# Offset weight buffers, earlier gating-norm loads and a later sample scaling in a one-layer decoder step

## The chip, the cores and the metric

The kernel runs on one core of one Trainium2 chip. The metric is device time in microseconds (us) of one execution. The kernel before has a median of 1687.88 us over three runs, which lie between 1686.46 and 1689.45 us. The profile comes from one more execution of the same program. In that execution the clock granted to TensorE is full throughout (0.999 in the mean).

In this text PE is TensorE, DVE is VectorE, ACT is ScalarE, POOL is GpSimd and SP is SyncE, whose queue issues most transfers. PEld is the weight-load half of TensorE. A queue name with a q, such as SPq, means the issuing of transfers on that engine.

## What is computed

The reference is one inference step of a decoder layer on 256 prompt positions and 8 sample positions, so 264 columns in all, with model width 4096. Cut to what matters here:

```
hn = rmsnorm(x, norm_gain)
p  = hn @ w_in                              # 4096 x 13324, split into 14 parts
A  = sink_attention(...) * silu(az)         # sliding window, 12 heads
B  = mlstm(...)  * sigmoid(mo) * silu(mz)   # 6 heads, matrix state
vv = layernorm(gelu(cv), c_ln_gain, c_ln_bias)
C  = gelu(cu) * (tril(w_s) @ vv + b_s) * silu(cz)
h  = x + concat(A, B, C) @ w_out            # 4096 x 4096
y  = rmsnorm(h, final_gain)                 # for the prompt and for the samples
cv_rows = vv of the last chunk              # an output of its own
```

The outputs are `y` for prompt and samples, the key and value rows, the mLSTM states, and the normalised rows `vv` of the last chunk, with scale and bias applied. All data is float32.

## The kernel before

**The matrix products.** The activations stand in SBUF as 32 rows of 264 values (one row for each 128 of the 4096 features), and they are split into a rounded part `xh` and a remainder `xl` (lines 129 and 130). Each row of `xh` and `xl` is padded from 264 to 320 values (`ROW`), which is 1280 bytes; `XOFF` is 0. The weights come in pieces of two 128x512 blocks (512 KB), also split into a rounded part `wh` and a remainder `wl`. Every product is made of three matmuls, `xh*wh`, `xl*wh` and `xh*wl`, with 128x128 weights and 264 columns. One step takes one 512 KB piece: four output blocks times two blocks of depth times three matmuls are 24 matmuls. Sixteen steps make a group of four output blocks. There are 26 groups for `w_in` and 8 for `w_out`, so 34 x 16 x 24 = 13056 main matmuls.

**How a weight piece gets there.** `load_w(n)` (line 219) issues the load of the float32 piece `wf` on SP's queue, four steps ahead. `split_w(n)` (line 228), two steps ahead, lets ACT copy it to `wh` and lets DVE subtract to give `wl`, with both of DVE's inputs in SBUF. There are three buffers each for `wf`, `wh` and `wl`. In the built program all `wh` and `wl` buffers and the rows of `xh` and `xl` start at multiples of 256 bytes in a partition, and the 128 columns of weights that one matmul takes are 512 bytes.

**What runs beside.** The rest (attention, mLSTM heads, gating, norms) is written as generators. Line 1000 starts the loop over all steps; before each output block `tick()` resumes such generators as their due times come. A due time is a `yield` with a number of microseconds, counted on a clock that the program keeps while it is written out, with estimated costs per instruction (lines 155 to 208). So the order on each engine is fixed when the program is built. Line 206 records every compute instruction, which is why nearly all rows of the profile say L206; tiles tell them apart.

**The gating part.** `gmlp_prep` (line 738) runs when the `cv` groups, the last two of `w_in`, begin. `gmlp_ln` (line 779) normalises the rows in `TM`, forms the eight gated blocks, and puts the residual `xt` back into `yb` by loads on SP's queue (lines 808, 809; line 1017 does the same for the other blocks). After that it loads the norm's scale and bias, broadcast to 128 partitions, 512 KB each, into `gb` (lines 810 to 812). POOL multiplies and adds them onto 128 and then 8 rows of `TM` (lines 815, 816), and SP's queue stores the results `o_cvp` and `o_cvs` (line 818). `gb` shares its memory with `rw`, which `gmlp_prep` uses.

**The end.** After the last matmul the sums of squares are reduced over partitions by small matmuls into `ns` (prompt) and `nss` (samples), from three tiles: `acc`, which POOL accumulates, and `last[0]` and `last[1]`, the squares of the last two blocks. `rsqrt` (line 270) is one DVE operation, a square root on ACT, and `newton`, four more on DVE. Then, for eight column blocks q, PE transposes `yb` (`turn`), ACT and DVE scale the two halves into `yo` (`put`), and SP's queue stores them (`store`). `state` and `state_out` write the mLSTM states in between. At q == 2 the samples' factor `rs` is formed and the scaled samples `yos` are stored, by SP's queue (lines 1118 to 1122).

Of the kernel before, what the change touches and what calls it, by code (L numbers as in the profile page):

```python
# [18 lines left out]
P = 128  # L19
# [50 lines left out]
LAG = 6.0  # L70
NCH = KT // KK
ROW = 320
XOFF = 0
PAD0, PAD1 = 32, 24

SM = {}
# [15 lines left out]
def body(tc, xt, wi, wg, wo, sm, kc, vc, c0, wst, w00, bs, cgain, cbias,  # L92
# [3 lines left out]
    with ExitStack() as ctx:  # L96
# [29 lines left out]
        keep = Phase("keep")  # L126

        cp.tile([P, PAD0], F32, name="pad0")
        xh = cp.tile([P, KT, ROW], F32R, name="xh")[:, :, XOFF:XOFF + T]
        xl = cp.tile([P, KT, ROW], F32R, name="xl")[:, :, XOFF:XOFF + T]  # L130
        yb = cp.tile([P, KT, T], F32, name="yb")
        sms = cp.tile([P, NSM], F32, name="sms")
        ones = cp.tile([P, P], F32, name="ones")
# [18 lines left out]
        def tt(eng, out, a, b, op):  # L152
            eng.tensor_tensor(out, a, b, op)
# [74 lines left out]
        def split_w(n):  # L228
            if n >= len(steps):
                return  # L230
            t = wf_t.pop(n)
            hi = wp.tile([P, KK, 512], F32R, name="wh")
            lo = wp.tile([P, KK, 512], F32R, name="wl")
            cur[0] = [None, clk["P"]]
            for sl in ((slice(0, 1), slice(1, 2)) if n == 0 else (slice(0, KK),)):
                A.activation(hi[:, sl], t[:, sl], AF.Copy)
                tt(V, lo[:, sl], t[:, sl], hi[:, sl].bitcast(F32), ALU.subtract)
            cur[0] = None
            wh_t[n], wl_t[n] = hi, lo
# [498 lines left out]
        def gmlp_prep():  # L738
            wm = ph.tile([P, CG, P], F32, name="wm")
            Z = ph.tile([P, CG, P], F32, name="Z")  # L740
            w0 = ph.tile([TS, CG], F32, name="w0")
            wI = ph.tile([TS, CG, TS], F32, name="wI")
            DQ.dma_start(wm, wst)
            DQ.dma_start(Z, bs.rearrange("(o g) t -> o g t", o=1).broadcast_to([P, CG, P]))
            DQ.dma_start(w0, w00.broadcast_to([TS, CG]))
            yield 6.0
            G.affine_select(out=wm, in_=wm, pattern=[[0, CG], [1, P]], compare_op=ALU.is_ge,
                            fill=0.0, base=0, channel_multiplier=-1)
            tt(V, wI, ident[:TS, :TS].unsqueeze(1).broadcast_to([TS, CG, TS]),
               w0.unsqueeze(2).broadcast_to([TS, CG, TS]), ALU.mult)  # L750
            yield
            rw = ph.tile([P, CG, P], F32, name="rw", tag="rg")
            nc.gpsimd.partition_all_reduce(rw, wm, P, ReduceOp.add)
            yield 12.0
            for g in range(CG):
                V.scalar_tensor_tensor(Z[:, g], rw[:, g], sc("cb", g), Z[:, g], ALU.mult, ALU.add)
                if g % 2:
                    yield
            st.update(wm=wm, Z=Z, wI=wI)

        def gmlp_tr(i):
            while ("gl", 4 * i + 3) not in st:
# [16 lines left out]
        def gmlp_ln():  # L779
            TM, bst, wm, Z, wI = [st[n] for n in ("TM", "bst", "wm", "Z", "wI")]  # L780
            mv = ph.tile([P, 5, 3], F32, name="mvs")
            for bb, n in ((slice(0, 2), P), (slice(2, 3), TS)):
                for b in range(bb.start, bb.stop):
                    V.bn_aggr(mv[:n, 0:2, b], bst[:n, b])
                rsqrt(mv[:n, 2, bb], mv[:n, 1, bb], 1.0, mv[:n, 3, bb], mv[:n, 4, bb])
                for b in range(bb.start, bb.stop):
                    V.tensor_scalar(TM[:n, b], TM[:n, b], mv[:n, 0, b:b + 1], mv[:n, 2, b:b + 1],
                                    ALU.subtract, ALU.mult)
            yield
            for g in range(CG):  # L790
                ps = yield from acq()
                sl = slice(P * g, P * g + P)
                PE.matmul(ps[:, 0:P], TM[:, 0, sl], wm[:, g], start=True, stop=True)
                PE.matmul(ps[:, P:TP], TM[:, 1, sl], wm[:, g], start=True, stop=True)
                PE.matmul(ps[:, TP:T], TM[:TS, 2, sl], wI[:, g], start=True, stop=True)
                s = ph.tile([P, T], F32, name="sg_s")
                V.scalar_tensor_tensor(s[:, :TP].rearrange("p (b t) -> p b t", b=2),
                                       ps[:, :TP].rearrange("p (b t) -> p b t", b=2), sc("cg", g),
                                       Z[:, g].unsqueeze(1).broadcast_to([P, 2, P]), ALU.mult, ALU.add)
                V.scalar_tensor_tensor(s[:, TP:], ps[:, TP:T], sc("cg", g),  # L800
                                       Z[:, g, 0:1].broadcast_to([P, TS]), ALU.mult, ALU.add)
                tt(V, yb[:, S_C + g], yb[:, S_C + g], s, ALU.mult)
                rel()
                split_y(S_C + g)
                st["c", g] = True
                yield NOW
                if g > 0:
                    DQ.dma_start(yb[:, S_C + g - 1, :], xt[:, S_C + g - 1, :])
            DQ.dma_start(yb[:, S_C + g, :], xt[:, S_C + g, :])
            gb = ph.tile([P, 2, 1024], F32, name="gb", tag="rg")  # L810
            DQ.dma_start(gb[:, 0], cgain.broadcast_to([P, 1024]))
            DQ.dma_start(gb[:, 1], cbias.broadcast_to([P, 1024]))
            yield 6.0
            for b, n, dst in ((1, P, o_cvp), (2, TS, o_cvs)):
                tt(G, TM[:n, b], TM[:n, b], gb[:n, 0], ALU.mult)
                tt(G, TM[:n, b], TM[:n, b], gb[:n, 1], ALU.add)
                yield
                DQ.dma_start(dst, TM[:n, b])


# [265 lines left out]
        def store(q, b, n):  # L1086
            sl = slice(512 * q, 512 * (q + n))
            DQ.dma_start(o_y[b, :, sl], yo[:, b, sl])

        turn(0, 0)  # L1090
        ns = pn.tile([P, 512], F32, name="ns", tag="sn")
        parts = [acc[:, 0]] + last
        for i, a in enumerate(parts):
            for b in range(2):
                PE.matmul(ns[:, b:b + 1], a[:, P * b:P * b + P], ones[:, 0:1], start=(i == 0 and b == 0),
                          stop=(i == len(parts) - 1), skip_group_check=True)
        r = hp.tile([P, 3, 2], F32, name="rn")
        rsqrt(r[:, 0], ns[:, :2], 1.0 / D, r[:, 1], r[:, 2])
        turn(0, 1)
        turn(1, 0)  # L1100
# [4 lines left out]
        for q in range(NGO):  # L1105
            for b in range(2):
                put(q, b)
                if q < 2 or q == NGO - 1:
                    store(q, b, 1)
                elif q in (3, 5):  # L1110
                    store(q - 1, b, 2)
                elif q == NGO - 2:
                    store(q, b, 1)
            if q >= 2:
                state_out(q - 2)
            if q < 2:
                final_gain(KT - 2 + q)
            if q == 2:
                rs = hp.tile([P, 3, TS], F32, name="rs")
                rsqrt(rs[:, 0], nss[:, :TS], 1.0 / D, rs[:, 1], rs[:, 2])  # L1120
                tt(V, yos, yb[:, :, TP:], rs[:, 0].unsqueeze(1).broadcast_to([P, KT, TS]), ALU.mult)
                DQ.dma_start(o_ys, yos)
            if q + 2 < NGO:
                turn(q + 2, 0)
                turn(q + 2, 1)
# [102 lines left out]
```

## Time and profile before

| what | us |
|---|---|
| median of three runs | 1687.88 |
| the profiled execution | 1685.23 |
| its span, first to last instruction | 1683.5 |
| PE busy in the span | 1670.5 |
| PEld busy | 1652.4 |
| DVE busy | 901.8 |
| ACT busy | 743.5 |
| POOL busy | 73.2 |

The span is 1.73 us shorter than the time of the profiled execution, which is what lies before the first and behind the last instruction. The profiled execution is 2.65 us below the median. A matmul's busy time is modelled and overlaps with the next, so the useful number for PE is how many matmuls it starts in a stretch. In the tables by stretch, the number after x counts every instruction that touches the stretch. Instructions are named as out<-in, with buffer numbers left out. In the timeline a bracket at the end of a row gives the idle time of the engine before the instruction and what ended it.

### The profile page before, as it was taken

Reading aid. Unit: us, or ns where it says so; the run is one execution under the profiler, and the core shown is the slowest. Engines: PE = TensorE matmul, PEld = TensorE weight load, DVE = VectorE, ACT = ScalarE, POOL = GpSimd, SP = SyncE. Lnnn points to the kernel's source line nnn. Section 1 sums busy time; section 2 is a strip of 40 time slices with the busy share of each in tenths; the row PEclk is TensorE's granted clock in tenths of the full one; section 3 lists DMA queues with packets and bytes.
Section 4 is the critical chain, followed back from the end, with each engine's and each line's share of the span. In section 5 each row is a group of like instructions: output and inputs, shape, how many; then the busy total and the mean of one; then the engine's idle time right before and its main releaser. Section 6 shows DMA issues by size and latency. Waiting matters only on the chain.

```text
span 1683.5 us, 32684 instructions
## 1 busy us (share of the span) xinstructions
PE 1670.5 (99%) x13830; PEld 1652.4 (98%) x13830; DVE 901.8 (54%) x1268; ACT 743.5 (44%) x979; POOL 73.2 (4%) x74
## 2 busy tenths in 40 slices
PE   9999999999999999999999999999999999999998
PEld 9999999999999999999999999999999999999997
DVE  6565644655544455555665656444666554444443
ACT  6554433444433433344444444434354443444443
POOL 0000000000000000011001100000100030000000
PEclk9999999999999999999999999999999999999999
DMA  8555668545455655667667666555656666555554
GB/s 300 172 183 175 184 188 277 158 158 165 153 172 180 184 181 185 204 204 241 220 222 238 220 219 223 180 184 181 208 176 217 201 200 195 182 187 178 186 178 159
DMA packets 102372, 328.94 MB, mean 195 GB/s; under 512 B 11155, under 2 KB 23753, under 8 KB 102225
## 3 DMA queue, kind: packets, MB, share of 16 engines
q1 hardware_dynamic: 101648, 326.04, 60.8%
q8 instruction: 108, 1.77, 0.4%
q10 hardware_dynamic: 576, 0.81, 0.1%
q14 instruction: 40, 0.32, 0.0%
HBM read 314.20 MB, written 12.60 MB: 194 GB/s over the span
## 4 chain that ended last, share of the span: by engine, by line
PE 96%; DVE 1%; DMA 1%; ACT 1%; issue 0%; SPq 0%; POOLq 0%; POOL 0%; DVEq 0%; ACTq 0%
PE mp L206 92%; PE mx L206 3%; DVE wl L206 1%; DMA wf<-wo 1%; DMA wf<-wi 0%; PE sn L206 0%; ACT wh L206 0%; PE gps L206 0%; DVE TM L206 0%; PE ns L206 0%; ACT es L206 0%; DVE yb L206 0%; DVE mvs L206 0%; ACT L206 0%; ACT yo L206 0%
## 5 line engine op out<-in xcount | busy, mean ns | idle before, releaser
L206 PE MATMUL mp<-xh,wh 128*128 128x264 f32 x4352 | 1242.7, 286 | 1.4 <-ACT wh L206 0.8
L206 PE MATMUL mp<-xh,wl 128*128 128x264 f32 x4352 | 1232.3, 283 | 3.1 <-DVE wl L206 3.1
L206 PE MATMUL mp<-xl,wh 128*128 128x264 f32 x4352 | 1231.5, 283 | 0.0
L206 DVE TENSOR_TENSOR wl<-wf,wh 128x1024 fp32r<-128x1024 f32 (+1 forms) x545 | 686.9, 1264 | 740.3 <-ACT wh L206 731.3
L206 ACT ACTIVATE wh<-wf 128x1024 fp32r<-128x1024 f32 (+1 forms) x545 | 574.7, 1057 | 807.3 <-PE mp L206 720.4
L206 PEld LDWEIGHTS mp<-xh,wh 128*128 128x128 f32 x4352 | 819.4, 188 | 8.7 <-issue 5.5
L206 PEld LDWEIGHTS mp<-xh,wl 128*128 128x128 f32 x4352 | 819.4, 188 | 4.6 <-DVE wl L206 4.6
L206 PEld LDWEIGHTS mp<-xl,wh 128*128 128x128 f32 x4352 | 819.7, 188 | 0.4
L206 POOL TENSOR_TENSOR acc<-acc,es 128x264 f32<-128x264 f32 x29 | 21.9, 754 | 412.9 <-ACT es L206 410.8
L206 ACT ACT_TABLE_LOAD x22 | 28.2, 1283 | 1.2 <-PEq L1208 0.8
L206 POOL TENSOR_SCALAR_AFFINE_SELECT tmp<-bc 128x128 f32<-128x128 f32 x12 | 5.6, 486 | 490.9 <-DMA bc<-gd 490.9
L206 ACT ACTIVATE es<-yb 128x264 f32<-128x264 f32 x37 | 15.2, 412 | 17.7 <-DVE yb L206 17.7
L206 ACT ACTIVATE bias<-bias,ar 128x128 f32<-128x128 f32 (+1 forms) x24 | 10.7, 448 | 25.0 <-DVE ar L206 24.9
L206 POOL TENSOR_TENSOR cb<-cb,bc 128x2056 f32<-128x2056 f32 x6 | 21.7, 3615 | 0.0
L206 ACT ACTIVATE es<-et 128x264 f32<-128x264 f32 x32 | 12.6, 419 | 17.1 <-DVE yb L206 13.8
L206 DVE SCALAR_TENSOR_TENSOR cb<-vb,wsk,cb 128x257 f32<-128x257 f32 x48 | 20.1, 481 | 0.0
L206 ACT ACTIVATE xh<-yb 128x264 fp32r<-128x264 f32 x32 | 12.1, 412 | 17.7 <-DVE yb L206 17.7
L206 POOL MEMSET pad<- 128x1024 f32 x2 | 1.9, 952 | 410.0 <-PE mx L206 410.0
L206 DVE TENSOR_TENSOR et<-mp,rstd 128x264 f32<-128x264 f32 x52 | 18.8, 425 | 0.0
L206 ACT ACTIVATE yb<-yb,sms 128x264 f32<-128x264 f32 x32 | 16.5, 516 | 0.9
L206 DVE SCALAR_TENSOR_TENSOR xl<-yb,sms,xh 128x264 fp32r<-128x264 f32 x32 | 14.4, 488 | 1.3 <-ACT xh L206 1.2
L206 DVE TENSOR_TENSOR xl<-yb,xh 128x264 fp32r<-128x264 f32 x32 | 12.7, 429 | 3.9 <-ACT xh L206 3.9
(195 smaller groups left out, 474.5 us busy)
## 6 DMA issues: line engine op xcount, KB each, us to landing
wf<-wi SPq DMA_DIRECT2D x415, 512.0 KB, 3.3
wf<-wo SPq DMA_DIRECT2D x128, 512.0 KB, 3.3
cb<-c SPq DMA_DIRECT2D x12, 514.0 KB
o_cs<-cb SPq DMA_DIRECT2D x12, 514.0 KB, 6.4
vb<-vsd SPq DMA_DIRECT2D x12, 512.0 KB, 4.5
yb<-xt SPq DMA_DIRECT2D x34, 132.0 KB, 3.5
yb<-xt SPq DMA_DIRECT2D x15, 264.0 KB, 7.0
Kc<-kc SPq DMA_DIRECT2D x4, 512.0 KB
```

The source lines that it names most:

```text
L206: return fn(*a, **k)
```

## The change

It has four parts.

- **Buffers of the weights.** Each `wh` and `wl` buffer gets 64 values (256 bytes) more, and the weights begin 30 values (`WOFF`), 120 bytes, into it. The buffers themselves still start at multiples of 256 bytes, so each slice of 128 columns now starts 120 bytes behind one. The padding of `xh` and `xl` stays. To make room, the scratch space for transfers shrinks from 1024 to 512 bytes, and the small tiles `rn` and `rs` move to another pool; all later tiles shift in memory.
- **Scale and bias of the gating norm.** `gb` no longer shares memory with `rw`. Its two loads move from the end of `gmlp_ln` to the end of `gmlp_prep`, each after a due time of 6 us. The four POOL operations get a due time of 12 us each ahead of them, and the stores one of 6 us.
- **The sums of squares.** The order of the three tiles becomes `last[0]`, `acc`, `last[1]`.
- **The samples' scaling.** The first two operations of its `rsqrt` go to q == 4, the rest with the multiplication to q == 5, and the store goes from SP's queue to ACT's.

```diff
-XOFF = 0
+WOFF = 30
...
-            hi = wp.tile([P, KK, 512], F32R, name="wh")
-            lo = wp.tile([P, KK, 512], F32R, name="wl")
+            hi, lo = [wp.tile([P, KK * 512 + 64], F32R, name=x)[:, WOFF:WOFF + KK * 512].rearrange(
+                "p (k c) -> p k c", k=KK) for x in ("wh", "wl")]
...
-            rw = ph.tile([P, CG, P], F32, name="rw", tag="rg")
+            rw = ph.tile([P, CG, P], F32, name="rw")
...
+            gb = ph.tile([P, 2, 1024], F32, name="gb")
+            for i, src in enumerate((cgain, cbias)):
+                yield 6.0
+                DQ.dma_start(gb[:, i], src.broadcast_to([P, 1024]))
+            st.update(wm=wm, Z=Z, wI=wI, gb=gb)
...
-            gb = ph.tile([P, 2, 1024], F32, name="gb", tag="rg")
-            DQ.dma_start(gb[:, 0], cgain.broadcast_to([P, 1024]))
-            DQ.dma_start(gb[:, 1], cbias.broadcast_to([P, 1024]))
-            yield 6.0
+            gb = st["gb"]
             for b, n, dst in ((1, P, o_cvp), (2, TS, o_cvs)):
-                tt(G, TM[:n, b], TM[:n, b], gb[:n, 0], ALU.mult)
-                tt(G, TM[:n, b], TM[:n, b], gb[:n, 1], ALU.add)
-                yield
+                for i, op in enumerate((ALU.mult, ALU.add)):
+                    yield 12.0
+                    tt(G, TM[:n, b], TM[:n, b], gb[:n, i], op)
+                yield 6.0
                 DQ.dma_start(dst, TM[:n, b])
...
-        parts = [acc[:, 0]] + last
+        parts = [last[0], acc[:, 0], last[1]]
...
-            if q == 2:
-                rs = hp.tile([P, 3, TS], F32, name="rs")
-                rsqrt(rs[:, 0], nss[:, :TS], 1.0 / D, rs[:, 1], rs[:, 2])
+            if q == 4:
+                rs = ph.tile([P, 3, TS], F32, name="rs")
+                V.tensor_scalar(rs[:, 1], nss[:, :TS], -0.5 / D, -0.5 * EPS, ALU.mult, ALU.add)
+                A.activation(rs[:, 2], nss[:, :TS], AF.Sqrt, scale=1.0 / D, bias=epsc[:, 0:1])
+            if q == 5:
+                newton(rs[:, 0], rs[:, 1], rs[:, 2])
                 tt(V, yos, yb[:, :, TP:], rs[:, 0].unsqueeze(1).broadcast_to([P, KT, TS]), ALU.mult)
-                DQ.dma_start(o_ys, yos)
+                nc.scalar.dma_start(o_ys, yos)
...
-    nc = _bacc.Bacc("TRN2", target_bir_lowering=False, num_devices=1, dynamic_dma_scratch_size=1024)
+    nc = _bacc.Bacc("TRN2", target_bir_lowering=False, num_devices=1, dynamic_dma_scratch_size=512)
```

Three places show how the order moves. The first is SP's queue around the start of the `w_out` groups, where `wf<-wo` are the weight pieces, `yb<-xt` the residual, `gb` the norm's scale and bias, and `o_cvp`, `o_cvs` the two stores. Before:

```order
L808 DMA yb<-xt 128x264
L225 DMA wf<-wo 128x1024 x4
L808 DMA yb<-xt 128x264
L809 DMA yb<-xt 128x264
L811 DMA gb<-cgain 128x1024
L812 DMA gb<-cbias 128x1024
L225 DMA wf<-wo 128x1024 x5
L818 DMA o_cvp<-TM 128x1024
L225 DMA wf<-wo 128x1024 x2
L818 DMA o_cvs<-TM 8x1024
```

On the same queue of the changed program, from the last loads of `w_in` on, whose pieces are `wf<-wi`:

```order
L225 DMA wf<-wi 128x1024 x15
L762 DMA gb<-cgain 128x1024
L225 DMA wf<-wi 128x1024 x2
L762 DMA gb<-cbias 128x1024
L225 DMA wf<-wi 128x1024 x9
L225 DMA wf<-wo 128x1024 x5
```

The two loads of `gb` now stand among the last 26 loads of `w_in` pieces, two weight pieces apart, and no longer ahead of weight pieces of `w_out`.

The second place is POOL at the start of the `w_out` groups; `TM<-TM,gb` are the four operations that apply scale and bias, and `acc<-acc,es` the accumulation of squares after each group of `w_out`:

```order
 L206 TENSOR_TENSOR acc<-acc,es 128x264 x3
 L206 TENSOR_TENSOR TM<-TM,gb 128x1024 x2
+L206 TENSOR_TENSOR acc<-acc,es 128x264 x4
 L206 TENSOR_TENSOR TM<-TM,gb 8x1024 x2
-L206 TENSOR_TENSOR acc<-acc,es 128x264 x26
-L1214 UNCONDITIONAL_BRANCH
-L1214 ISA
+L206 TENSOR_TENSOR acc<-acc,es 128x264 x22
```

The two operations on 128 rows stay ahead of the second group's sums; the two on 8 rows move behind them.

The third place is DVE in the end phase, where `yo` are the scaled output blocks, `rs` the samples' factor and `yos` the scaled samples:

```order
-L206 TENSOR_SCALAR yo<-mp,rn 128x512 x3
+L206 TENSOR_SCALAR yo<-mp,rn 128x512 x5
 L206 TENSOR_SCALAR rs<-mx 128x8
+L206 TENSOR_SCALAR yo<-mp,rn 128x512
 L206 RECIPROCAL rs<-rs 128x8
 L206 TENSOR_TENSOR rs<-rs 128x8 x2
 L206 SCALAR_TENSOR_TENSOR rs<-rs 128x8
 L206 TENSOR_TENSOR yos<-yb,rs 128x256
-L206 TENSOR_SCALAR yo<-mp,rn 128x512 x5
-L1214 UNCONDITIONAL_BRANCH
+L206 TENSOR_SCALAR yo<-mp,rn 128x512 x2
```

Three more output blocks now stand ahead of the reciprocal, and two instead of five behind the multiplication. PE's order has no difference that these names show.

More of the change, by code (lines that the diff above doesn't have):

```diff
@@ L128, in body @@
         cp.tile([P, PAD0], F32, name="pad0")
-        xh = cp.tile([P, KT, ROW], F32R, name="xh")[:, :, XOFF:XOFF + T]
-        xl = cp.tile([P, KT, ROW], F32R, name="xl")[:, :, XOFF:XOFF + T]
+        xh = cp.tile([P, KT, ROW], F32R, name="xh")[:, :, :T]
+        xl = cp.tile([P, KT, ROW], F32R, name="xl")[:, :, :T]
         yb = cp.tile([P, KT, T], F32, name="yb")
@@ L758, in gmlp_prep @@
                     yield
-            st.update(wm=wm, Z=Z, wI=wI)
+            gb = ph.tile([P, 2, 1024], F32, name="gb")
[3 more added lines that the diff above has]
+            st.update(wm=wm, Z=Z, wI=wI, gb=gb)
         def gmlp_tr(i):
@@ L1096, in body @@
                           stop=(i == len(parts) - 1), skip_group_check=True)
-        r = hp.tile([P, 3, 2], F32, name="rn")
+        r = ph.tile([P, 3, 2], F32, name="rn")
         rsqrt(r[:, 0], ns[:, :2], 1.0 / D, r[:, 1], r[:, 2])
@@ L1107, in body @@
                 put(q, b)
-                if q < 2 or q == NGO - 1:
-                    store(q, b, 1)
-                elif q in (3, 5):
+                if q in (3, 5):
                     store(q - 1, b, 2)
-                elif q == NGO - 2:
+                elif q not in (2, 4):
                     store(q, b, 1)
```

## The prediction

> **What bounds the kernel now.** I began with the page: its span, its busy times and the chain that ended last.
>
> ```profile
> span 1683.5 us, 32684 instructions
> PE 1670.5 (99%) x13830; PEld 1652.4 (98%) x13830; DVE 901.8 (54%) x1268; ACT 743.5 (44%) x979; POOL 73.2 (4%) x74
> PEclk9999999999999999999999999999999999999999
> PE 96%; DVE 1%; DMA 1%; ACT 1%; issue 0%; SPq 0%; POOLq 0%; POOL 0%; DVEq 0%; ACTq 0%
> L206 PE MATMUL mp<-xh,wh 128*128 128x264 f32 x4352 | 1242.7, 286 | 1.4 <-ACT wh L206 0.8
> ```
>
> TensorE carries 96% of the chain, its clock is full throughout, and and the first kind of main matmul, `xh*wh`, runs 4352 times and waits 1.4 us in all; the other two kinds look alike. So only two things can move the time by much: how far apart consecutive main matmuls start, and the few places where TensorE stands still. Busy times don't tell the first, since matmuls overlap. I took it from the chain's longest piece, which holds nothing but main matmuls, and from a table by stretch of TensorE's main matmuls alone, one stretch inside each of five consecutive groups (columns: busy and count, clock, DMA share, GB/s).
>
> ```profile
> 478.14 262.11 PE mp L206 x2172
> ...
> 507.00:552.00 45.00, 45.00 (x373) 1.00 0.60 185
> 553.00:598.00 45.00, 45.00 (x377) 1.00 0.60 185
> 599.00:644.00 45.00, 45.00 (x377) 1.00 0.59 183
> 646.00:691.00 45.00, 45.00 (x374) 1.00 0.59 184
> 692.00:737.00 45.00, 45.00 (x377) 1.00 0.64 209
> ```
>
> The piece gives 262.11 / 2172 = 120.7 ns from one start to the next, short pauses between groups included. In the table, 45 us plus the 0.29 us that a matmul lasts (286 ns above), since the count takes in all that touch the stretch, over the count, is 120.1 ns in three groups and 121.2 ns in the other two. The same instructions, with the same tile sizes and buffers, have two rhythms, and a group keeps its rhythm to the end. So the spacing is not set by the amount of work alone, but also by how weight loads and matmuls fall against each other.
>
> How far down could it go? A row of the groups gives one weight load of the main loop, and two rows of the end phase show what TensorE does when it streams less:
>
> ```profile
> L206 PEld LDWEIGHTS mp<-xh,wl 128*128 128x128 f32 x4352 | 819.4, 188 | 4.6 <-DVE wl L206 4.6
> ...
> 1662.32 0.53 PEld L206 LDWEIGHTS ns<-ones,et 128*128 128x128 f32 x4
> ...
> 1672.40 0.87 PE mp L206 x8
> ```
>
> The second row is four loads of 128 columns of weights, each ahead of a matmul of one column. With 188 ns for a single load they recur every (530 - 188) / 3 = 114 ns. The main loop's 120.7 ns are 6.7 ns above that. The third row is eight transposes at 109 ns each. Their moving operand, the identity, begins 616 bytes into `sms`, which is 8 bytes off a multiple of 16, and that doesn't slow them.
>
> The stalls come next. This table by stretch has all engines; TensorE's count is the first.
>
> ```profile
> core 0: us, PE busy (x) PEld busy (x) DVE busy (x) ACT busy (x) POOL busy (x), PEclk, DMA share, GB/s
> 1240.00:1280.00 40.00, 40.00 (x331) 40.00 (x331) 25.63 (x39) 21.61 (x37) 0.00 (x0) 1.00 0.58 179
> 1340.00:1360.00 20.00, 18.04 (x144) 17.21 (x143) 11.40 (x7) 5.50 (x6) 11.35 (x4) 1.00 0.76 231
> 1360.00:1380.00 20.00, 20.00 (x167) 20.00 (x166) 9.19 (x8) 7.57 (x8) 0.00 (x0) 1.00 0.71 231
> ```
>
> Between 1340 and 1360 us TensorE starts 23 matmuls fewer than in the stretch behind, 23 x 0.12 = 2.7 us. The timeline tells why:
>
> ```profile
> 1340.33 0.43 SPq L811 DMA_DIRECT2D gb<-cgain  x1
> 1340.80 0.43 SPq L812 DMA_DIRECT2D gb<-cbias  x1
> ...
> 1350.08 2.26 ACT L206 ACTIVATE wh<-wf 128x1024 fp32r<-128x1024 f32 x2 [6.48 <-DMA wf<-wo]
> ...
> 1346.89 11.50 POOL L206 TENSOR_TENSOR TM<-TM,gb 128x1024 f32<-128x1024 f32 x4 [9.78 <-DMA gb<-cgain]
> ...
> 1343.63 1.23 DVE L206 TENSOR_TENSOR wl<-wf,wh 128x1024 fp32r<-128x1024 f32 x1 [2.17 <-ACT wh L206]
> 1351.17 9.45 DVE L206 TENSOR_TENSOR wl<-wf,wh 128x1024 fp32r<-128x1024 f32 x4 [6.31 <-ACT wh L206]
> ...
> 1352.88 0.39 PE L206 MATMUL mp<-xh,wl 128*128 128x264 f32 x1 [1.19 <-DVE wl L206]
> ```
>
> The two loads of `gb` stand ahead of the next weight piece on SP's queue, and ACT waits 6.48 us for it. Then POOL's four operations lie side by side with four subtractions on DVE, which take 9.45 us instead of 4 x 1.23. Both make `wl` late, and TensorE waits for it.
>
> **The change part by part, gating norm.** The `gb` loads leave this place, so the weight pieces follow each other, and the POOL operations come 12 us of program time apart, one beside one or two subtractions instead of four beside four. I count the whole stall as gone: -2.7 us. The bounds are 0, if either cause alone keeps it, and -2.7. What is late next there is nothing the trace shows: in the stretch behind, TensorE is full. The moved loads are 2 x 512 KB among weight pieces of the last `w_in` groups, where the transfers are busy 0.58 of the time and TensorE is full, and pieces are issued four steps ahead. I cost them at nothing; if that cover failed, each would delay a piece by no more than its own transfer, 1.4 us at the 370 GB/s of the row of rates below, so +2.8 us for both. The spread POOL operations cost nothing as long as a subtraction may be 2.2 us late (the longest less the median in this row of the `wl` tile from 1340 to 1362 us), which lies inside a step of 24 x 0.12 = 2.9 us; the splits run two steps ahead.
>
> ```profile
> L206 DVE TENSOR_TENSOR wl<-wf,wh x8: 1212/1226/3411, 1338.9 to 1361.5; 128x1024 fp32r<-128x1024 f32 x8
> ```
>
> **The end.** Here are rows of the timeline of the last 24 us, and the transfer shares and rates in 40 slices of 0.6 us from 1660 us on.
>
> ```profile
> 1661.88 0.61 PE L206 MATMUL ns<-ones,acc 128*128 128x1 f32 x4 [0.17 <-POOL acc L206]
> ...
> 1668.74 0.69 ACT L206 ACTIVATE yo<-mp,rn 128x512 f32<-128x512 f32 x1
> ...
> 1668.89 0.20 DVE L206 RECIPROCAL rs<-rs 128x8 f32<-128x8 f32 x1 [1.50 <-ACT rs L206]
> ...
> 1670.07 2.25 DVE L206 TENSOR_SCALAR yo<-mp,rn 128x512 f32<-128x512 f32 x3
> 1670.18 0.33 SPq L1122 DMA_DIRECT2D o_ys<-yos  x1
> ...
> 1670.62 8.72 SPq L1088 DMA_DIRECT2D o_y<-yo  x8
> ...
> 1676.21 0.68 ACT L206 ACTIVATE yo<-mp,rn 128x512 f32<-128x512 f32 x1
> ...
> DMA  0000000000599991006999999999999999970000
> GB/s 0 0 0 0 0 27 0 0 0 0 218 379 372 386 376 31 0 0 213 399 420 382 417 403 423 382 396 417 379 370 386 379 370 383 379 280 14 0 0 0
> ```
>
> From about 1671 us to 1682 us transfers run without a break at 370 to 423 GB/s, and the last `yo` is finished at 1676.9 us: the end is bound by transfers, and what counts is when they resume. ACT has its block of q = 3 at 1669.43 us, but DVE sits 1.50 us on the samples' factor with its own block behind it, and SP's queue holds the blocks' stores behind `o_ys`, until 1670.62 us. With the factor later and `o_ys` on ACT's queue the stores can go 1.19 us earlier. The new order of the sums lets PE start on `last[0]` while POOL still adds, which saves about the 0.17 us of that wait. Together -1.4 us. On ACT's queue, `o_ys` now waits for DVE's `yos` ahead of ACT's next `yo`. I cost that at nothing, because about 5 us of stored-up transfers cover it; without that cover it is one factor chain, +1.5 us, so the bounds are -1.4 and +0.1.
>
> **The weights' offset.** It adds no instruction. ACT and DVE write to shifted addresses, off the path: ACT is busy 44% of the span. What it may change is the spacing. Now all operands of a main matmul start at multiples of 256 bytes; then only the activations do. No row has a main matmul with shifted weights, so I bound it. Downwards it is the 114 ns of weight loads alone: 13056 x 6.7 ns = -87 us. Upwards it is a longer weight load, worked out as a rival below. In between lies the 120.1 ns rhythm, which the same loop reaches in three groups of five. I take that value, because it is the nearest row of the same instructions: 13056 x 0.6 ns = -8 us. The reason to expect a gain at all is that one rhythm of two drifts, and that the offset shifts one of two streams against the other in every matmul alike.
>
> The Trainium skill speaks against the offset in "SBUF — State Buffer", section "Specifications (TRN2)": memory lines are 16 bytes, and each step to a new line costs. By that page a slice of 512 bytes touches 33 lines instead of 32, so my estimate from it is a load of 114 x 33/32 = 117.6 ns, still shorter than 120.7, and the sum stays. No row here has weights off a line.
>
> **Sum.** The profiled execution took 1685.23 us: 1685.23 - 2.7 - 1.4 - 8 = 1673.1 us. It lies 2.65 us below the median of 1687.88, so against the median I forecast 1675.8, rounded to 1676 us.
>
> **Rivals.** *No effect of the offset.* Weight loads and matmuls may meet nowhere in memory, and both rhythms may come from TensorE's own hand-over. For it speaks that every slice of 512 bytes of a buffer gives the same rhythm; against it, that all those slices have the same start within 256 bytes, so the trace never tried another. Then 1687.88 - 4.1 = 1683.8 us. The Trainium skill is on this side in "SBUF — State Buffer", section "Who interferes with whom": TensorE reads moving operand and weights through independent ports and waits for no one. By it the offset changes nothing; two rhythms at one set of addresses neither confirm nor refute it.
>
> *A deep gain.* If most of the 6.7 ns comes from the two reads meeting, and the offset parts them, the time goes below 1640 us, at best to 1687.88 - 4.1 - 87 = 1597 us. Against it: the two rhythms differ by only 1.1 ns. In the Trainium skill, "TensorE: Matmul & The Clock Gate", section "Back-to-back issue gap", 264 columns take 264/2.4 + 2.5 = 112.5 ns. The trace's 120.1 is above that, and by the page's figure the best case would be 1577 us.
>
> *Slower: a longer weight load.* A slice that starts between boundaries may fetch one piece more, in all 13056 matmuls. It decides once the load exceeds the spacing, 120.7 / 114, or 6% more: with pieces of 32 bytes (17 for 16) it would just reach 121 ns and cost little, with pieces of 64 bytes (9 for 8) it becomes 128 ns, 13056 x 7.5 = +98 us, so 1687.88 - 4.1 + 98 = 1782 us. For it: the weight load is busy 98% beside PE. Against it: the transposes with an operand off a line at 109 ns, though that is the moving one.
>
> **How the numbers follow.** I give the forecast 0.38 (1640 to 1682 us), no effect 0.34 (1681 to 1688), the deep gain 0.10, the slower case 0.18. A measurement of this kernel can tell about 0.2% from no change, here 3.4 us, so the bounds are 1684.5 and 1691.3 us. No effect at 1683.8 lies on the edge, half of it on either side: faster is 0.38 + 0.10 + 0.17 = 0.65; the other half and 0.02 of mild losses are 0.19 within; 0.16 is slower. The range from 1640 to 1696 us holds the forecast, no effect, and some 0.09 of the two outer cases, about 0.81.
>
> **What would show it.** In stretches of 45 us inside groups the count should be 377 nearly everywhere; 373 as often as now means no effect, 380 and more the deep gain, 370 and less the longer load. The stretch of 20 us at the start of the `w_out` groups should reach some 167, with single subtractions of 2 to 3.5 us beside POOL. In the end phase the first store of the eight should follow ACT's `yo` of q = 3 within 0.1 us. I am wrong if the spacing stays and the time falls by more than 7 us, or if a stall appears where `gb` now loads.

## The result, and the profile after

The changed kernel has a median of 1712.99 us over four runs (1709.98 to 1718.66), the kernel before beside it 1688.6 us. The ratio is 1.015, 95% interval 1.0122 to 1.0179: slower by 24 us, where I had forecast 1676 us and a range up to 1696 us.

The page of the changed kernel comes from an execution of 1713.0 us. Of it I read the span, the busy times, the granted clock, the chain that ended last and the first two kinds of main matmul.

```profile
span 1711.3 us, 32682 instructions
PE 1698.7 (99%) x13830; PEld 1681.4 (98%) x13830; DVE 905.1 (53%) x1268; ACT 743.4 (43%) x979; POOL 73.8 (4%) x74
...
PEclk9999999999999999999999999999999999999999
...
PE 97%; DVE 1%; ACT 0%; DMA 0%; issue 0%; SPq 0%; ACTq 0%; DVEq 0%
...
L206 PE MATMUL mp<-xh,wh 128*128 128x264 f32 x4352 | 1256.3, 289 | 1.4 <-ACT wh L206 0.8
L206 PE MATMUL mp<-xh,wl 128*128 128x264 f32 x4352 | 1245.8, 286 | 3.2 <-DVE wl L206 2.9
```

The span is 27.8 us longer. TensorE still carries the chain, at full clock, and its waits are still a few us. The loss must lie in the spacing, and the table by stretch of TensorE's main matmuls shows it (length, busy and count, clock, DMA share, GB/s):

```profile
517.00:562.00 45.00, 45.00 (x378) 1.00 0.59 185
563.00:608.00 45.00, 45.00 (x377) 1.00 0.58 185
...
655.00:700.00 45.00, 45.00 (x377) 1.00 0.60 187
701.00:746.00 45.00, 45.00 (x364) 1.00 0.62 200
1105.00:1150.00 45.00, 45.00 (x364) 1.00 0.57 177
1546.00:1591.00 45.00, 45.00 (x364) 1.00 0.55 176
```

There are again two rhythms. The fast one is as before: 45 us plus the length of a matmul (0.29 us), over the count, is 45.29 / 377 = 120.1 ns. The slow one has grown from 121.2 to 45.29 / 364 = 124.4 ns. Over the whole trace (the mean over the spacings of main matmuls that follow each other, pauses above 145 ns left out) the spacing went from 120.70 to 122.93 ns. Averaged by steps of 24 matmuls, 263 steps were fast (below 120.7 ns) and 278 slow before, and 174 are fast and 367 slow now. 13056 x 2.23 ns = 29 us, a little more than the 27.8 us by which the span grew, so this is the whole loss.

A group need not keep its rhythm. Two stretches inside one group of the changed kernel:

```profile
159.00:171.00 12.00, 12.00 (x98) 1.00 0.47 144
174.00:203.00 29.00, 29.00 (x244) 1.00 0.58 182
```

The first has 12.29 / 98 = 125 ns within the accuracy of so short a count, the second 29.29 / 244 = 120.0 ns.

### The profile page after: what moved, and what is told of

Its sections match the earlier page's. It is cut to its first block, busy times and chain, and to the rows that moved or that the text cites. A ratio compares the mean times of both kernels' runs of the same rounds, so it can differ in the third digit from the quotient of the medians.

```text
span 1711.3 us, 32682 instructions
## 1 busy us (share of the span) xinstructions
PE 1698.7 (99%) x13830; PEld 1681.4 (98%) x13830; DVE 905.1 (53%) x1268; ACT 743.4 (43%) x979; POOL 73.8 (4%) x74
## 4 chain that ended last, share of the span: by engine, by line
PE 97%; DVE 1%; ACT 0%; DMA 0%; issue 0%; SPq 0%; ACTq 0%; DVEq 0%
PE mp L206 93%; PE mx L206 3%; DVE wl L206 1%; DMA wf<-wi 0%; PE sn L206 0%; PE gps L206 0%; ACT wh L206 0%; DVE TM L206 0%; ACT yo L206 0%; DVE mvs L206 0%; PE ns L206 0%; ACT L206 0%; ACT co L206 0%; DVE rn L206 0%; SPq L987 0%
## 5 line engine op out<-in xcount | busy, mean ns | idle before, releaser
L206 PE MATMUL mp<-xh,wh 128*128 128x264 f32 x4352 | 1256.3, 289 | 1.4 <-ACT wh L206 0.8
L206 PE MATMUL mp<-xh,wl 128*128 128x264 f32 x4352 | 1245.8, 286 | 3.2 <-DVE wl L206 2.9
L206 DVE TENSOR_TENSOR yb<-mp,yb 128x264 f32<-128x264 f32 x32 | 11.8, 424 | 5.5 <-PE mp L206 5.5
```

Of the source, the lines that this page charges most:

```text
L206: return fn(*a, **k)
```

## The experiments

From here on, "rows" are the activation rows `xh` and `xl`, "distance" is the start of the weights less the start of the rows, modulo 256 bytes, and "slow rhythm" is the mean spacing in the slow steps. A "line" is a multiple of 16 bytes. The fast rhythm is 120.0 ns wherever there is one. Edits are against the changed kernel unless something else is said, and one `WOFF` is 4 bytes. The times are medians; each ratio is against the kernel before, run beside it.

**Is it the offset?** Two runs take it from both sides. The first keeps all but the offset:

```diff
-WOFF = 30
+WOFF = 0
```

> The changed kernel with the weights at byte 0 of their buffers; buffers still 256 bytes longer, everything else as changed. Theory L (weight slices that start off a 16-byte line make the slower rhythm of the matmuls longer) and theory R (the distance between the starts of weights and activation rows makes it longer) both expect the slower rhythm back at about 121.3 ns and 1688 us: 1688.6 for before, less 0.9 us at the end, plus 0.4 us of stalls at the start of the w_out groups. Theory O (something else of the change: buffer spacing, shifted memory, order) expects it to stay at 124.4 ns and 1713 us.

The second puts the offset alone, with the room that it needs, into the kernel before:

```diff
+WOFF = 30
-            hi = wp.tile([P, KK, 512], F32R, name="wh")
-            lo = wp.tile([P, KK, 512], F32R, name="wl")
+            hi, lo = [wp.tile([P, KK * 512 + 64], F32R, name=x)[:, WOFF:WOFF + KK * 512].rearrange(
+                "p (k c) -> p k c", k=KK) for x in ("wh", "wl")]
...
-        r = hp.tile([P, 3, 2], F32, name="rn")
+        r = ph.tile([P, 3, 2], F32, name="rn")
...
```

> The kernel before with only the offset of 120 bytes and the buffers' 256 bytes more (with the smaller scratch space and the two small tiles moved, which make room). L and R: slower rhythm 124.4 ns, about 1714 us. O: 121.3 ns, about 1688 us.

Without the offset: 1684.88 us, 0.9994 [0.9984, 1.0003]. With the offset alone: 1718.58 us, 1.019 [1.0162, 1.0218]. In TensorE's main matmuls the run without the offset is back at the counts of the kernel before, and the run with the offset alone has those of the changed kernel:

```profile
517.00:562.00 45.00, 45.00 (x372) 1.00 0.62 179
```

```profile
517.00:562.00 45.00, 45.00 (x377) 1.00 0.63 182
...
1105.00:1150.00 45.00, 45.00 (x364) 1.00 0.60 176
```

So the loss comes from the offset. The other parts of the change, which I had forecast at -4.1 us together, brought about 1 us in the run without the offset (the interval is from -2.7 to +0.5 us).

**A line of 16 bytes, or the distance?** 112 bytes lie on a 16-byte line, 120 do not:

```diff
-WOFF = 30
+WOFF = 28
```

> The changed kernel with an offset of 112 bytes instead of 120, a multiple of 16. L: the slices start on a line again, slower rhythm 121.3 ns, about 1688 us. R: nearly the same distance as with 120 bytes, slower rhythm about 124 ns, about 1713 us.

The next run shifts the rows by the same 120 bytes as the weights, so that the distance is 0 again:

```diff
-        xh = cp.tile([P, KT, ROW], F32R, name="xh")[:, :, :T]
-        xl = cp.tile([P, KT, ROW], F32R, name="xl")[:, :, :T]
+        xh = cp.tile([P, KT, ROW], F32R, name="xh")[:, :, WOFF:WOFF + T]
+        xl = cp.tile([P, KT, ROW], F32R, name="xl")[:, :, WOFF:WOFF + T]
```

> The changed kernel with the rows of xh and xl also begun 120 bytes behind a multiple of 256, so that weights and rows have distance zero again, both off a 16-byte line. R: slower rhythm 121.3 ns, about 1688 us. L: 124.4 ns or more, 1713 us or more.

112 bytes: 1709.04 us, 1.0138 [1.0121, 1.0155], with most slow steps at 124.45 ns and the others at 121.4. Both at 120 bytes: 1729.98 us, 1.026 [1.0244, 1.0275], slow rhythm 125.0 ns in seven steps of eight. The line alone can't be it, since 112 bytes cost nearly as much; the distance alone can't either, since distance 0 is the worst so far.

**How the cost runs over the offset.** Four runs at other places:

```diff
-WOFF = 30
+WOFF = 32
```

> The changed kernel with an offset of 128 bytes. Theory B: a slice of weights that starts off a multiple of some size B takes one piece more, and only the slower rhythm shows it; 112 and 120 bytes exclude B = 16. B of 32, 64 or 128: slower rhythm 121.3 ns, about 1685 us as without an offset. B = 256: 124.4 ns, about 1710 us. Rival P (any offset disturbs how the buffers stand to each other, not the boundary): 124.4 ns, about 1710 us.

```diff
-WOFF = 30
+WOFF = 16
```

> Offset of 64 bytes. B of 32 or 64: 121.3 ns, about 1685 us. B of 128 or 256, or P: 124.4 ns, about 1710 us.

```diff
-WOFF = 30
+WOFF = 8
```

> Offset of 32 bytes. B = 32: 121.3 ns, about 1685 us. B of 64, 128 or 256, or P: 124.4 ns, about 1710 us.

And the rows at 120 bytes with unshifted weights:

```diff
-WOFF = 30
+WOFF = 0
-        xh = cp.tile([P, KT, ROW], F32R, name="xh")[:, :, :T]
+        xh = cp.tile([P, KT, ROW], F32R, name="xh")[:, :, 30:30 + T]
...
```

> The weights without an offset, the rows of xh and xl begun 120 bytes behind a multiple of 256 instead. If the streamed operand counts pieces too, a slower rhythm between 121.3 and 125.0 ns (125.0 was that of both shifted) and a time between 1685 and 1730 us; if only weight loads are tight, 121.3 ns and about 1685 us; if the distance of the two counts after all, about as with the weights shifted, 124.4 ns and 1710 us.

128 bytes: 1696.33 us, 1.0059 [1.0039, 1.0079]. 64 bytes: 1679.46 us, 0.9957 [0.9942, 0.9972]. 32 bytes: 1677.47 us, 0.9949 [0.993, 0.9969]. Rows at 120: 1737.19 us, 1.0305 [1.0285, 1.0325]. The table by stretch with the weights at 32 bytes, then that with the rows at 120:

```profile
517.00:562.00 45.00, 45.00 (x377) 1.00 0.62 179
...
1105.00:1150.00 45.00, 45.00 (x376) 1.00 0.63 186
1546.00:1591.00 45.00, 45.00 (x377) 1.00 0.61 179
```

```profile
517.00:562.00 45.00, 45.00 (x362) 1.00 0.60 176
...
1546.00:1591.00 45.00, 45.00 (x362) 1.00 0.58 176
```

The first has 120.1 to 120.5 ns everywhere, the second 125.1 ns everywhere. So an offset can do what I forecast for it, at 32 and 64 bytes, and the opposite at 112, 120 and 128. No single boundary size explains that 32 and 64 are better than 0 while 128 is worse: none of the theories put up had a rhythm below 121.3 ns at 32 or 64, 128 fell between the two, and the rows at 120 came out above the range given for them.

**Own place, or distance to the rows?** 96 bytes fill the gap:

```diff
-WOFF = 30
+WOFF = 24
```

> Weights 96 bytes into their buffers, activation rows where they were. If the cost rises smoothly from 64 bytes on (second rhythm 120.0 at 64, 124.45 at 112 and 120), this lies between: second rhythm about 122 to 123, 1685 to 1700 us. If only the place inside 64 bytes counts (32 and 96 alike), it is like 32 bytes: 120.0 everywhere, about 1677.5 us.

Two more put the rows 64 bytes in, on a line, with distances 0 and 32; this is the first, and the second has `WOFF = 24`:

```diff
-WOFF = 30
+WOFF = 16
-        xh = cp.tile([P, KT, ROW], F32R, name="xh")[:, :, :T]
+        xh = cp.tile([P, KT, ROW], F32R, name="xh")[:, :, 16:16 + T]
...
```

> Weights and activation rows both 64 bytes in, so that their distance is 0 as in the kernel before. If only the distance of the two counts as long as the rows start on a multiple of 16 bytes, it is like no offset at all: rhythms of 120.0 and 121.3, about 1685 us. If the weights' own place counts, it is like 64 bytes with unmoved rows: 120.0 nearly everywhere, about 1679.5 us. If any shift of the rows is what costs (125.0 with rows at 120 bytes), it is above 1720 us.

> Activation rows 64 bytes in, weights 96 bytes in, so that the weights are 32 bytes behind the rows as in the run that had 120.0 everywhere. If the distance counts, 120.0 everywhere and about 1677.5 us. If the weights' own place counts, it is like 96 bytes with unmoved rows. If any shift of the rows costs, above 1720 us.

Weights at 96, rows unmoved: 1697.47 us, 1.0062 [1.0048, 1.0075], every step slow at 121.7 ns, a little under the rhythm expected. Both at 64: 1684.68 us, 0.9989 [0.998, 0.9998], rhythms of 120.0 and 121.3 as with no offset at all. Rows at 64, weights at 96: 1677.6 us, 0.9943 [0.9929, 0.9957]. The same place of the weights, 96 bytes, first with unmoved rows and then with rows at 64, in the tables by stretch:

```profile
1105.00:1150.00 45.00, 45.00 (x372) 1.00 0.63 185
```

```profile
1105.00:1150.00 45.00, 45.00 (x376) 1.00 0.62 182
1546.00:1591.00 45.00, 45.00 (x377) 1.00 0.61 186
```

Moving the rows alone takes the slow rhythm away. With rows and weights on lines the distance counts, not the weights' own place: distance 0 gave the same at two places, and so did distance 32.

**And the line?** Three runs try to separate it from the distance: weights at 40 bytes, 8 off a line like 120 but near the good distances; rows at 112 and weights at 144, both on lines with distance 32; rows at 8 and weights at 40, both off a line with distance 32. A fourth tries the distance 192.

```diff
-WOFF = 30
+WOFF = 10
```

> Weights 40 bytes in, which is 8 bytes off a line of 16 bytes, as 120 bytes is, but near the distances 32 and 64 that had 120.0 ns everywhere. If only the distance between weights and rows counts, 120.0 everywhere and about 1677.5 us. If a start off a 16-byte line costs by itself, a second rhythm of 121 ns or more appears and the time is above 1685 us.

```diff
-WOFF = 30
+WOFF = 36
-        xh = cp.tile([P, KT, ROW], F32R, name="xh")[:, :, :T]
+        xh = cp.tile([P, KT, ROW], F32R, name="xh")[:, :, 28:28 + T]
...
```

> Activation rows 112 bytes in and weights 144 bytes in: the rows on a 16-byte line, the distance 32 bytes. If the rows at 120 bytes cost because they start off a 16-byte line (there 125.0 ns everywhere), and otherwise the distance counts, this has 120.0 everywhere and about 1677.5 us. If rows near the middle of 256 bytes cost by their place, it has about 125 ns and 1725 us or more.

```diff
-WOFF = 30
+WOFF = 48
```

> Weights 192 bytes in, rows unmoved: the distance is 192, or 64 the other way round. If the cost is one hump over the distance around 112 to 128 bytes, symmetric in 256, it is like 64 bytes: 120.0 nearly everywhere, about 1679.5 us. If it grows with the distance, or goes in steps that repeat, it is at or above the 123.3 ns of 128 bytes, 1696 us or more.

```diff
-WOFF = 30
+WOFF = 10
-        xh = cp.tile([P, KT, ROW], F32R, name="xh")[:, :, :T]
+        xh = cp.tile([P, KT, ROW], F32R, name="xh")[:, :, 2:2 + T]
...
```

> Activation rows 8 bytes in, weights 40 bytes in: both 8 bytes off a 16-byte line, their distance 32 bytes. If the 125.0 ns with rows at 120 bytes come from the rows' start off a line, this has about 125.0 everywhere and 1730 to 1740 us. If the distance alone counts, 120.0 everywhere and about 1677.5 us. If weights and rows off a line by the same amount cost no more than weights alone did at 40 bytes, 121.3 and about 1692 us.

Weights at 40: 1692.47 us, 1.0033 [1.0021, 1.0046], every step slow at 121.3 ns, 1.3 ns above 32 bytes. Rows at 112, weights at 144: 1677.56 us, 0.9944 [0.993, 0.9957], 120.0 ns. Distance 192: 1685.95 us, 0.9995 [0.9986, 1.0004], slow rhythm 121.0 ns, which fits neither of the two theories put up for it. Rows at 8, weights at 40: 1737.31 us, 1.0305 [1.0288, 1.0323]. The tables by stretch for weights at 40, rows at 112 and rows at 8, in this order:

```profile
1105.00:1150.00 45.00, 45.00 (x373) 1.00 0.63 185
```

```profile
1105.00:1150.00 45.00, 45.00 (x377) 1.00 0.63 181
```

```profile
1105.00:1150.00 45.00, 45.00 (x362) 1.00 0.60 175
```

So both count. Rows 8 bytes off a line give 125.0 ns at all three distances tried, 0, 32 and 136 (all steps in two runs, seven of eight in the third). For the rows the 16 bytes come out of the runs themselves: starts at 0, 64 and 112 are free of this, 8 and 120 are not. Weights at 40 bytes cost 1.3 ns more than at 32; whether that is the line or the distance 40 these runs can't tell, because with rows on a line any distance that is no multiple of 16 puts the weights off a line. At 120 bytes the line adds nothing to be seen: 124.3 ns, and 124.45 at 112. With rows and weights on lines, the distance sets the slow rhythm. All runs that bear on it:

| rows at, weights at (bytes) | distance | fast and slow steps | slow rhythm, ns |
|---|---|---|---|
| 0, 0 (offset removed) | 0 | 220, 320 | 121.3 |
| 64, 64 | 0 | 260, 280 | 121.3 |
| 0, 32 | 32 | 534, 7 | – |
| 64, 96 | 32 | 539, 2 | – |
| 112, 144 | 32 | 533, 8 | – |
| 0, 64 | 64 | 464, 77 | 121.5 |
| 0, 96 | 96 | 0, 541 | 121.7 |
| 0, 112 | 112 | 145, 395 | 121.4 and 124.45 |
| 0, 128 | 128 | 289, 252 | 123.3 |
| 0, 192 | 192 | 119, 422 | 121.0 |
| 0, 40 (off a line) | 40 | 0, 541 | 121.3 |
| 0, 120 (off a line; the changed kernel) | 120 | 174, 367 | 124.3 |
| 8, 40 (both off) | 32 | 0, 541 | 125.0 |
| 120, 120 (both off) | 0 | 66, 475 | 125.0 |
| 120, 0 (rows off) | 136 | 0, 541 | 125.0 |

**The gating norm.** Its stall did not go, so two runs with the weights at 32 bytes ask why. In the first, each of POOL's four operations waits until a later group of `w_out` is written out:

```diff
-WOFF = 30
+WOFF = 8
...
-                    yield 12.0
+                    while ("out", 2 * b - 2 + i) not in st:
+                        yield 3.0
...
                         evac_out(4 * (g - NG) + j, out)
+                        st["out", g - NG] = j == 3
```

> The weights begin 32 bytes into their buffers, and each of the four GpSimd operations on the gating rows waits until a later group of w_out has been written out, so that it stands singly between the accumulations. If the double stall of 3.2 us in the changed kernel comes from pairs of these operations running side by side with the subtractions, single ones leave nearly no gap at the first 100 us of w_out and the time falls to about 1674.5 us, 3 us below the 1677.5 of the 32-byte run. If one operation alone is enough to make a subtraction late, four gaps of up to 1.4 us stay and the time is about 1677.5 or above.

It took 1677.29 us, 0.9945 [0.9931, 0.9958], no better than 32 bytes alone, as the second half of the expectation has it. The operations do stand singly now, but each still comes right at a group's end, and there is a stall at each of the four. At the first, at 1331 us, a single operation is enough to stretch the subtraction beside it to 2.81 us. The second comes another way:

```profile
1375.72 2.41 POOL L206 TENSOR_TENSOR TM<-TM,gb 128x1024 f32<-128x1024 f32 x1
...
1378.07 2.43 POOL L206 TENSOR_TENSOR acc<-acc,es 128x264 f32<-128x264 f32 x3
1378.86 0.42 ACT L206 ACTIVATE es<-yb 128x264 f32<-128x264 f32 x1 [1.73 <-POOL acc L206]
...
1380.81 3.50 DVE L206 TENSOR_TENSOR wl<-wf,wh 128x1024 fp32r<-128x1024 f32 x3 [5.46 <-ACT wh L206]
```

POOL's accumulations queue behind its `TM` operation, ACT's squares `es` wait 1.73 us for them, and behind the squares on ACT stands `wh`, which `wl` needs. The second run leaves the due times as the change has them and gives the four operations to VectorE:

```diff
-WOFF = 30
+WOFF = 8
...
-                    tt(G, TM[:n, b], TM[:n, b], gb[:n, i], op)
+                    tt(V, TM[:n, b], TM[:n, b], gb[:n, i], op)
```

> Weights 32 bytes in, and the four operations of the gating norm on VectorE instead of GpSimd, with the same due times of 12 us. If the two stalls come from GpSimd running its operations at a group's end, where the subtractions have least slack, they go: no gap of TensorE over 0.33 us from 1300 us on up to the last main matmul except the one at the end of w_in, and about 1674.5 us, 3 us below the 1677.5 of the 32-byte run. If any fifth kind of work beside the subtractions makes them late, or the due times do not space VectorE either, gaps of about 1 us stay and the time is 1676.5 or more.

It took 1674.25 us, 0.9925 [0.9911, 0.9938], with a span of 1671.8 us against 1674.4 for 32 bytes alone (the two intervals overlap, so the profile has to carry the difference). Its table by stretch (TensorE's busy time and count first) and its timeline of DVE:

```profile
1340.00:1360.00 20.00, 20.00 (x169) 20.00 (x168) 9.72 (x8) 8.29 (x8) 0.00 (x0) 1.00 0.67 190
1360.00:1380.00 20.00, 20.00 (x168) 19.97 (x167) 10.78 (x12) 10.40 (x16) 3.02 (x4) 1.00 0.58 181
1380.00:1400.00 20.00, 20.00 (x169) 20.00 (x168) 9.91 (x9) 7.28 (x8) 0.00 (x0) 1.00 0.68 212
```

```profile
1346.86 1.22 DVE L206 TENSOR_TENSOR TM<-TM,gb 128x1024 f32<-128x1024 f32 x1
1348.59 1.23 DVE L206 TENSOR_TENSOR wl<-wf,wh 128x1024 fp32r<-128x1024 f32 x1 [0.52 <-ACT wh L206]
...
1364.13 1.22 DVE L206 TENSOR_TENSOR TM<-TM,gb 128x1024 f32<-128x1024 f32 x1
1365.87 1.23 DVE L206 TENSOR_TENSOR wl<-wf,wh 128x1024 fp32r<-128x1024 f32 x1 [0.52 <-ACT wh L206]
```

The stall is gone, all stretches are full, and the two operations lie 17 us apart inside a group, each finished before the next `wh` is ready. From 1300 us on, successive main matmuls start at most 0.25 us apart, which is within what I expected. This is the fastest kernel of the study, 0.75% below the kernel before.

## Why the prediction was wrong, point by point

**What bounds the kernel** held: spacing and a few stalls, nothing else. That "a group keeps its rhythm to the end" did not hold. It is true of the five groups that I looked at; averaged by steps, 14 of the 34 groups before and 9 after have at least two steps of either rhythm.

**The weights' offset: the step that failed.** I bounded the unknown between -87 and +98 us and then took "the 120.1 ns rhythm", -8 us, "because it is the nearest row of the same instructions". That row showed what the loop can reach, not that this offset reaches it; the very same argument holds for any offset, and the runs show it to be right for the rhythm at 32 and nearly so at 64 bytes (120.05 and 120.23 ns in the mean over the trace, against 120.1 forecast) and wrong at 120. A row of the kernel before could not tell these apart, because all its main matmuls have the distance 0. The honest use of it would have been a chance near even for both signs. In its place stands +29 us: the fast rhythm stays, and the slow one becomes longer (124.3 ns) and more frequent. The rival of no effect falls with the run of the offset alone. The two other parts, worked out below, came to about +0.5 and -0.9 us. Nothing of the deep gain showed: in no run did a rhythm go below 120.0 ns.

**The rival of a longer weight load** had the right side, but the runs speak against its mechanism. Its sign was to be counts of 370 and less, and 364 came; but a longer load in every matmul would have left no stretch at 377, an offset of 32 or 64 bytes could not have gained, and the load's own duration hardly moved, from 188 ns to 189 in this row of the groups of the changed kernel:

```profile
L206 PEld LDWEIGHTS mp<-xh,wh 128*128 128x128 f32 x4352 | 824.5, 189 | 7.8 <-issue 5.1
```

I argued against it with the transposes, whose moving operand starts 8 bytes off a line without harm. The main matmuls don't behave so: with the rows 8 bytes off a line they go at 125.0 ns. The witness was another kind of matmul.

The rule of 16-byte lines ("SBUF — State Buffer", section "Specifications (TRN2)", of the Trainium skill) points the right way: 5 ns for rows off a line, and 1.3 ns for weights at 40 bytes if the line is the cause there. It says nothing that would explain 124.45 ns at 112 bytes, which lie on a line. By section "Who interferes with whom" of the same page of the Trainium skill, the two reads of TensorE go through independent ports. That alone would leave no room for the distance, but moving only the rows from 0 to 64 bytes took 121.7 ns back to 120.0.

**The gating norm** was costed at -2.7 us; it brought nothing. The moved `gb` loads went as forecast: they are issued at 1247 and 1253 us, and TensorE waits for nothing from 1240 to 1300 us. But "12 us of program time apart" is not 12 us apart on the chip. The table by stretch of the changed kernel, and its timelines of POOL and of DVE:

```profile
1340.00:1360.00 20.00, 19.70 (x157) 19.20 (x156) 11.46 (x18) 10.84 (x18) 4.85 (x5) 1.00 0.44 145
1360.00:1380.00 20.00, 19.09 (x156) 18.87 (x157) 11.77 (x9) 6.79 (x7) 3.03 (x1) 1.00 0.66 209
1380.00:1400.00 20.00, 20.00 (x169) 20.00 (x168) 8.42 (x8) 7.42 (x7) 0.00 (x0) 1.00 0.60 180
1400.00:1420.00 20.00, 18.71 (x151) 18.27 (x150) 12.90 (x11) 9.57 (x14) 8.62 (x6) 1.00 0.58 193
1420.00:1440.00 20.00, 20.00 (x163) 20.00 (x162) 7.72 (x7) 7.39 (x7) 0.00 (x0) 1.00 0.56 177
```

```profile
1354.81 0.76 POOL L206 TENSOR_TENSOR acc<-acc,es 128x264 f32<-128x264 f32 x1 [131.78 <-ACT es L206]
...
1357.31 5.72 POOL L206 TENSOR_TENSOR TM<-TM,gb 128x1024 f32<-128x1024 f32 x2
...
1405.30 5.71 POOL L206 TENSOR_TENSOR TM<-TM,gb 8x1024 f32<-8x1024 f32 x2
```

```profile
1357.99 7.26 DVE L206 TENSOR_TENSOR wl<-wf,wh 128x1024 fp32r<-128x1024 f32 x3 [3.66 <-ACT wh L206]
...
1405.97 8.47 DVE L206 TENSOR_TENSOR wl<-wf,wh 128x1024 fp32r<-128x1024 f32 x4 [3.62 <-ACT wh L206]
```

A due time only fixes the order in which instructions are written. POOL's queue holds nothing between the accumulations, so it waits 131.78 us for the first of them and then runs both operations of a pair back to back, at a group's end. Of the three or four subtractions that follow each other there, the first two take 2.8 and 3.4 us instead of 1.23; the others, behind POOL's work, are as short as ever. Three of the stretches are short of matmuls. How much is lost can't be had from the counts, because the rhythm changes between them (169 from 1380 us on, 163 from 1420 us on, both undisturbed). In the trace the starts of TensorE's matmuls stand 1.43, 0.36, 1.40 and 0.45 us apart at these places; less a spacing each, that is 3.1 us, in two places, where the same count gives 2.6 us in one for the kernel before. So in place of -2.7 us stands +0.5. The order of POOL shown ahead of the prediction had the pairs in it. On VectorE, which gets its subtractions step by step, the same due times space the operations, and there they cost nothing.

**The end** brought 0.9 us of the 1.4: from the start of the last main matmul to the end of the span it takes 21.63 us, 22.52 before. In the changed kernel's timeline and its transfer shares and rates (40 slices of 0.6 us from 1688 us on):

```profile
1696.94 0.68 ACT L206 ACTIVATE yo<-mp,rn 128x512 f32<-128x512 f32 x1
...
1699.28 0.75 DVE L206 TENSOR_SCALAR yo<-mp,rn 128x512 f32<-128x512 f32 x1 [0.92 <-PE mp L206]
...
1700.15 0.39 ACT L206 ACTIVATE co<-mx 128x257 f32<-128x257 f32 x1 [0.25 <-PE mx L206]
1700.43 0.26 ACT L206 ACTIVATE rs<-mx,epsc 128x8 f32<-128x8 f32 x1
1700.58 0.69 ACT L206 ACTIVATE yo<-mp,rn 128x512 f32<-128x512 f32 x1
...
1701.30 0.81 SPq L1090 DMA_DIRECT2D o_y<-yo  x2
...
1702.75 0.63 ACTq L1125 DMA_DIRECT2D o_ys<-yos  x1
```

```profile
DMA  0000000100099996059999959999999999940000
GB/s 0 0 0 0 0 0 0 27 0 0 0 379 376 379 376 253 0 212 423 396 410 376 367 208 389 396 416 372 374 366 389 372 384 386 382 171 3 0 0 0
```

ACT has its block of q = 3 at 1697.62 us and transfers resume in the slice that begins at 1698.2, 8.6 us after the start of the last main matmul; before, they resumed 9.8 us after it (1670.8 us). So the wait for the samples is gone there: 1.2 us of the 1.4 forecast. But in the slice at 1701.8 us the rate falls to 208: the transfers run dry for about half a slice, 0.3 us. The stores of q = 4 and 5, issued from 1701.30 us on, wait for ACT's block of q = 5, which ends at 1701.27 us, while DVE's block of q = 5 was done at 1700.03. ACT came to it late because it waits for PE's state matmuls (`co`), and because the samples' square root (`rs`), which the change put just ahead of that block, moves it by another 0.15 us. I had counted on about 5 us of stored-up transfers as the cover; by then the transfers have run for 3.6 us and have used up what was finished. So the sum of the end was too large by a break at q = 5 that I had put at nothing. The store of the samples on ACT's queue cost nothing that the transfers show.

## What to carry to other kernels

When a loop of TensorE runs at a few ns per matmul above its best, try the starts of weights and activation rows against each other in several steps, with both on 16-byte lines, before believing any one offset: here 32 bytes brought 0.5% and 120 cost 1.5%. A bound taken from what the loop can reach says nothing on which side a change of addresses falls. A due time in the program spaces only an engine whose queue is otherwise held in step; on an idle queue it needs something that it truly waits for, or another engine.

## What the runs showed of the hardware

With 264 columns in the rounded 32-bit type (float32r) and 128x128 weights the spacing of matmuls depended on addresses: 120.0 ns at best, 125.0 ns when the activation rows began 8 bytes off a 16-byte line, and between 120.0 and 124.45 ns by the distance of weights and rows within 256 bytes. It is no single hump: in the slow steps distance 0 gave 121.3 ns, 32 bytes 120.0, 96 bytes 121.7, 112 bytes 124.45, 128 bytes 123.3 and 192 bytes 121.0. What in the chip makes it so stays open, and so does what sets the number of slow steps: at 40 and 96 bytes all were slow, at 112, 120 and 128 only some. GpSimd's operation took as long for 8 rows as for 128 (2.41 us each where it stood singly, and 5.71 and 5.72 us for two in a row). In the changed kernel a subtraction of VectorE that ran into them took 2.8 to 3.4 us instead of 1.23. They took turns: the first subtraction starts at 1357.99 us and ends at 1360.79, 1.08 us after the first GpSimd operation has ended, and the second ends 1.08 us after the second.
